# A decoder trunk's planned order of operations: new planner constants and a second queue for the first weight tile

## The chip, the cores and the metric

The kernel runs on one core of a Trainium2 chip. The metric is device microseconds of one execution, as the median of several runs. A core has TensorE (PE), VectorE (DVE), ScalarE (ACT), GpSimdE (POOL) and SyncE (SP), each with its own instruction queue that it works off in order, and transfer engines (DMA) that move data between memory and the core's own memory.

## The reference

256 tokens of width 1024 go through two layers. Each layer is a half-step SwiGLU feed-forward block, a token mixer and another half-step feed-forward block. The mixer of the first layer (A) is causal sliding-window attention with 16 query heads on 2 key heads, learned sinks and a relative-position bias; that of the second (B) is latent attention with low-rank queries and keys and a rotary part.

```python
def swiglu(h, wg, wu, wd):
    return (jax.nn.silu(h @ wg) * (h @ wu)) @ wd
...
    for i in range(DEPTH):
        x = x + 0.5 * swiglu(rmsnorm(x, ffn_norm1[i]), ffn1_wg[i], ffn1_wu[i], ffn1_wd[i])
        h = rmsnorm(x, mix_norm[i])
        j = i // N_MIXERS
        if i % N_MIXERS == 0:
            x = x + sliding_window_attention(h, positions, rel_bias, a_w_in[j], a_q_gain[j],
                                             a_k_gain[j], a_sinks[j], a_w_out[j])
        else:
            x = x + latent_attention(h, positions, b_w_in[j], b_q_norm[j], b_kv_norm[j],
                                     b_w_uq[j], b_w_ukv[j], b_q_gain[j], b_k_gain[j], b_w_out[j])
        x = x + 0.5 * swiglu(rmsnorm(x, ffn_norm2[i]), ffn2_wg[i], ffn2_wu[i], ffn2_wd[i])
```

All is float32; the hidden width of the feed-forward blocks is 2816.

## The kernel before, in words

The tokens stand as two tiles of 128 (t = 0 and 1). Weights come as tiles of 128 x 1024 float32 (512 KB) into `raw`, five buffers. Each is split into a high part `whi` (ScalarE, L402) and a low part `wlo` (VectorE, L397), eight buffers each; a product of two float32 matrices is then three matmuls in TensorE's rounded float32: high by high, high by low, low by high (L735 to L737 for projections, L783 for the down projection, L854 for gate and up). A feed-forward block runs in 11 chunks of 256 hidden columns: gate and up, tanh and products on ScalarE and VectorE, the cast `pT` and its rest `t` of the result, and the down projection of the chunk before. The cast of h (L868) may run on ScalarE or VectorE.

In layer A, keys and queries are projected, normalised (squares on ScalarE, a sum on VectorE, a power on GpSimdE, L647) and transposed (L688); then for each t, key head and parity come scores (L1063), a softmax (row maximum L896 and the scaling of p L941 on VectorE, exponentials L920 on ScalarE), transposes of p (L688), the product with v (L1089) and the output projection. Layer B does the same with its own lines: L1180 and L1209 make keys and queries, L1260 and L1262 scores, L1274 the product with v. The scaling of p may run on VectorE, GpSimdE or ScalarE.

No one writes the order by hand. The program first records every operation with its engine, an estimated cost, what it reads and writes (`Plan.op`), and then `Plan.run` orders them: at each step it takes, of all operations that are ready, the one with the earliest start by its model plus a penalty `pen`. `PEN` holds penalties by kind of operation and engine, `SKEW` how far t = 1 is put behind t = 0 in each stage, `WINDOW` how far in a stream it looks ahead, `PENW` the penalty of weight splits. `pe_time` models TensorE's clock: time is cut into ticks, and a tick runs at half rate where too little work was booked in the tick before. `o.dense` says how much an operation counts there (scores and products with v count for less). Where the plan leaves TensorE idle, `fill` puts filler matmuls of the identity (L1348), whose results nobody reads. The instructions stand in each engine's queue in the order found.

All weight transfers, and those of x (L345, two halves for each t), are issued from SP (L394). The first weight tile comes in two halves, each as two transfers: four in all.

Of the kernel before, what the change touches and what calls it, by code (L numbers as in the profile page):

```python
# [41 lines left out]
WINDOW = 20  # L42
RESERVE = 1
SKEW = [1, 7, 8, 3, 4, 2]
# [3 lines left out]
PENW = [1.0, 0.5, 0.7, 0.7, 0.6, 1.0]  # L48
PEN = {
    "C": {"DVE": -0.4, "POOL": -0.2},  # L50
    "CT": {"*": 0.05, "DVE": -0.1, "PE": -0.05},
    "G": {"DVE": -1},
    "KT": {"PE": 0.05},
    "KV": {"*": -0.2, "ACT": -0.1, "DVE": -0.1, "PE": 0.05},
    "N": {"ACT": 0.4, "DVE": -0.1, "PE": -0.05, "POOL": 0.2},
    "Oa": {"PE": -0.05},
    "PT": {"PE": -0.2},
    "PTB": {"*": 0.05, "PE": -0.6},
    "PV": {"*": -0.6, "DVE": -0.05, "PE": -0.2},
    "PVB": {"*": 0.6, "PE": 0.2},  # L60
    "Q": {"ACT": 0.1, "DVE": 0.1},
    "QB": {"PE": 0.4},
    "QTB": {"*": 0.1},
    "S": {"ACT": 0.1, "PE": -0.2},
    "SB": {"PE": 0.05},
    "T": {"*": -0.05, "PE": -0.1},
    "X": {"DVE": 0.4},
    "Xa": {"DVE": -0.1},
    "Xb": {"DVE": -0.2},
}  # L70
POOLPEN = 1
FILLMIN, FILLFROM = 0.5, 2.0
BSPEN = 2.0
# [27 lines left out]
class Plan:  # L101
# [22 lines left out]
    def op(self, eng, cost, fn, r=(), w=(), seq=None, pen=0.0, prio=None, tail=0.0, name=None):  # L124
# [29 lines left out]
        o.dense = 0.6 if nm[:1] in ("S", "P") and eng == "PE" and nm[1:2] != "T" else 1.0  # L154
# [64 lines left out]
    def pe_time(self, s, cost, book=False, dense=1.0):  # L219
# [87 lines left out]
def kernel(  # L307
# [24 lines left out]
    def c_act(n, extra=0.0):  # L332
        return 0.1 + 0.00083 * n + extra
# [43 lines left out]
    def weight(key, n, srcs):  # L377

        if key not in wtiles:
# [7 lines left out]
            for j in range(parts):  # L387
# [204 lines left out]
    def bias_ops(t, grp):  # L592
# [9 lines left out]
        for i0 in (0, 4) if t else ():  # L602
# [10 lines left out]
            op("ACT", 8 * c_act(P, 0.02), fn, [nj, qidx, df, hd], [m, (steps, i0)], pen=BSPEN, name="bs")  # L613
# [78 lines left out]
    def norm(t, key, gi):  # L692
# [11 lines left out]
        for hf in range(2):  # L704
# [4 lines left out]
            for k2 in (2 * hf, 2 * hf + 1):  # L709
# [12 lines left out]
                op(AV, (0.48, 0.4), high, [b, (gc, int(gi > 1))], xk(0, t, k2), name=name)  # L722
# [8 lines left out]
        op("POOL", 0.97, rs, [ss, mhalf], [rstd, var], name=name)  # L731
# [22 lines left out]
    def ffn(key, gi, wg, wu, wd, extra=None, last=False):  # L754
# [44 lines left out]
        def first(t):  # L799
# [8 lines left out]
            op("POOL", 0.35, consts, [rstd], [hr, q2], name=f"hr{key}.{t}")  # L808
# [29 lines left out]
        for c in range(1, NCH):  # L838
            hthi, htlo = ht[c] = buf("pT", [P, 2, NT * P], F32R), buf("t2", [P, 2, NT * P], F32R)
            for fb in range(2):  # L840
# [27 lines left out]
                op(AV, (c_act(FC, -0.05), c_dve(FC)), copy_scaled(lambda hthi=hthi, fb=fb: hthi[:, fb], lambda h=h: h.t),  # L868
# [233 lines left out]
    def mixer_b(t):  # L1102
# [98 lines left out]
        def queries(g):  # L1201
# [28 lines left out]
            op("DVE", 0.6, rope, [qb, K["ssq", t], K["ccq", t]], [(qn, 1), tmp], name=name)  # L1230
# [166 lines left out]
```

## Time and profile before

| | |
|---|---|
| three timed runs | 952.58, 953.30, 954.87 us; median 953.3 |
| the profiled execution | 955.77 us |
| its span, first to last instruction | 954.0 us |
| its mean granted TensorE clock | 0.994 |

The page of a profile gives busy times by engine and line. A window table gives, for a stretch of time, the busy time of each engine, the granted clock of TensorE as a share of 2.4 GHz, and what the transfers moved. A timeline lists instructions with start and duration, merged where the same one repeats, and in brackets how long the engine had been idle and what ended that. A float32 matmul whose operands are not rounded appears as two records for scores, fillers and keys. PE stands for matmuls, PEld for the loads of their stationary operand.

### The profile page before, as it was taken

Reading aid. Unit: us, or ns where it says so; the run is one execution under the profiler, and the core shown is the slowest. Engines: PE = TensorE matmul, PEld = TensorE weight load, DVE = VectorE, ACT = ScalarE, POOL = GpSimd, SP = SyncE. Lnnn points to the kernel's source line nnn. Section 1 sums busy time; section 2 is a strip of 40 time slices with the busy share of each in tenths; the row PEclk is TensorE's granted clock in tenths of the full one; section 3 lists DMA queues with packets and bytes.
Section 4 is the critical chain, followed back from the end, with each engine's and each line's share of the span. In section 5 each row is a group of like instructions: output and inputs, shape, how many; then the busy total and the mean of one; then the engine's idle time right before and its main releaser. Section 6 shows DMA issues by size and latency. Waiting matters only on the chain.

```text
span 954.0 us, 16706 instructions
## 1 busy us (share of the span) xinstructions
PE 940.6 (99%) x6378; PEld 842.6 (88%) x6378; DVE 654.8 (69%) x1283; ACT 490.4 (51%) x854; POOL 49.4 (5%) x117
## 2 busy tenths in 40 slices
PE   8999999999999999999999999999999999999998
PEld 6999999988668999999989999998868889999997
DVE  6787777786767765666686656566698677565662
ACT  7484666355556543544464434443587445344540
POOL 2000000013000000000010000000431000000000
PEclk9999999999799999999999999999999999999999
DMA  8766556545115666565655656656201477556441
GB/s 287 232 209 209 167 176 192 165 133 179 43 45 178 219 200 199 166 200 165 201 172 173 204 178 187 203 162 199 95 1 46 141 238 225 192 177 209 159 140 45
DMA packets 119632, 160.07 MB, mean 168 GB/s; under 512 B 9264, under 2 KB 102912, under 8 KB 119552
## 3 DMA queue, kind: packets, MB, share of 16 engines
q1 hardware_dynamic: 119552, 159.00, 53.2%
q8 instruction: 50, 0.82, 0.4%
q14 instruction: 30, 0.25, 0.1%
HBM read 157.92 MB, written 1.05 MB: 167 GB/s over the span
## 4 chain that ended last, share of the span: by engine, by line
PE 93%; DVE 3%; DMA 2%; ACT 1%; issue 1%; SPq 0%; POOL 0%; DVEq 0%; ACTq 0%
PE w L854 47%; PE acc L783 26%; PE w L688 3%; PE acc L735 2%; PE acc L737 2%; PE acc L736 2%; PE w L735 1%; PE w L737 1%; PE w L736 1%; DMA raw<-in_ffn_wu_dram 1%; DVE wlo L397 1%; PE w L1262 1%; PE w L1209 1%; PE w L1063 1%; PE acc L1089 1%; PE acc L1274 1%
## 5 line engine op out<-in xcount | busy, mean ns | idle before, releaser
L854 PE MATMUL w<-xs,whi 128*128 128x256 f32 x2560 | 458.3, 282 | 0.0
L854 PEld LDWEIGHTS w<-xs,whi 128*128 128x128 f32 x2560 | 395.4, 189 | 3.4 <-ACT whi L402 0.2
L397 DVE TENSOR_TENSOR wlo<-raw,whi 128x1024 fp32r<-128x1024 f32 (+2 forms) x295 | 352.4, 1215 | 53.1 <-ACT whi L402 50.0
L402 ACT CAST whi<-raw 128x1024 fp32r<-128x1024 f32 (+2 forms) x295 | 303.8, 1042 | 121.1 <-PE acc L783 68.1
L854 PE MATMUL w<-xs,wlo 128*128 128x256 f32 x1280 | 360.5, 282 | 0.8 <-DVE wlo L397 0.8
L854 PEld LDWEIGHTS w<-xs,wlo 128*128 128x128 f32 x1280 | 241.0, 188 | 1.0 <-DVE wlo L397 1.0
L862 ACT ACTIVATE th<-h 128x256 f32<-128x256 f32 x80 | 33.5, 419 | 202.6 <-DVE h L860 202.6
L783 PE MATMUL acc<-wlo,pT 128*128 128x512 f32 x352 | 113.5, 396 | 0.0
L783 PE MATMUL acc<-whi,pT 128*128 128x512 f32 x352 | 113.5, 396 | 0.0
L783 PE MATMUL acc<-whi,t 128*128 128x512 f32 x352 | 113.3, 396 | 0.0
L860 DVE TENSOR_TENSOR h<-w,rb 128x256 f32<-128x256 f32 x80 | 34.0, 424 | 112.3 <-PE w L854 111.2
L783 PEld LDWEIGHTS acc<-whi,t 128*128 128x128 f32 x352 | 66.1, 188 | 16.3
L783 PEld LDWEIGHTS acc<-wlo,pT 128*128 128x128 f32 x352 | 66.1, 188 | 15.4
L783 PEld LDWEIGHTS acc<-whi,pT 128*128 128x128 f32 x352 | 63.4, 189 | 12.0
L870 DVE TENSOR_TENSOR t<-h,pT 128x256 fp32r<-128x256 f32 x80 | 34.0, 425 | 28.4 <-ACT pT L656 27.6
L864 DVE SCALAR_TENSOR_TENSOR th<-th,w 128x256 f32<-128x256 f32 x80 | 33.5, 419 | 26.5 <-ACT th L862 26.5
L656 ACT CAST pT<-h 128x256 fp32r<-128x256 f32 x61 | 24.8, 406 | 32.2 <-DVE h L866 32.0
L735 PE MATMUL acc<-whi,xs 128*128 128x512 f32 x96 | 39.9, 415 | 0.1
L737 PE MATMUL acc<-whi,xs 128*128 128x512 f32 x96 | 38.2, 398 | 0.4 <-DVE xs L674 0.4
L736 PE MATMUL acc<-wlo,xs 128*128 128x512 f32 x96 | 37.8, 394 | 0.0
L920 ACT ACTIVATE p<-p,st 128x128 f32<-128x128 f32 (+1 forms) x64 | 31.2, 491 | 10.2 <-DVE st L911 6.6
L735 PE MATMUL w<-whi,xs 128*128 128x512 f32 (+2 forms) x96 | 36.2, 377 | 0.0
(190 smaller groups left out, 814.6 us busy)
## 6 DMA issues: line engine op xcount, KB each, us to landing
raw<-in_ffn_wd_dram SPq DMA_DIRECT2D x88, 512.0 KB, 4.7
raw<-in_ffn_wg_dram SPq DMA_DIRECT2D x175, 256.0 KB, 3.9
raw<-in_ffn_wu_dram SPq DMA_DIRECT2D x175, 256.0 KB, 4.3
raw<-in_a_w_in_dram SPq DMA_DIRECT2D x10, 512.0 KB, 4.5
raw<-in_a_w_out_dram SPq DMA_DIRECT2D x8, 512.0 KB, 4.1
raw<-in_b_w_out_dram SPq DMA_DIRECT2D x8, 512.0 KB, 3.8
raw<-in_b_w_in_dram SPq DMA_DIRECT2D x4, 416.0 KB, 3.5
whi<-in_b_w_uq_dram SPq DMA_DIRECT2D x4, 384.0 KB, 3.1
```

The costliest lines, as they stand in the source:

```text
L397: V.tensor_tensor(out=lo[:, c], in0=raw[:, c], in1=hi.t.bitcast(F32)[:, c], op=ALU.subtract)
L402: op("ACT", c_act(m), lambda c=c: A.copy(out=hi[:, c], in_=raw[:, c]), [(raw, key_)], [(hi, key_)], seq="wh", pen=pen, prio=pr, name="W")
L735: T.matmul(o, lhsT=hi, rhs=wh, start=start, stop=False)
L736: T.matmul(o, lhsT=hi, rhs=wl, start=False, stop=False)
L737: T.matmul(o, lhsT=lo, rhs=wh, start=False, stop=stop)
L783: T.matmul(acc[nh].t, lhsT=a[:, ft, t0 : t0 + P], rhs=wt[:, nh * 512 : (nh + 1) * 512], start=(c == 0 and ft == 0 and i == 0), stop=(final ...
L854: T.matmul(o, lhsT=wt[:, sl], rhs=xs[:, p, :, kt], start=(kt == j == i == 0), stop=(kt == KT - 1 and j == 1 and i == 2))
L860: op("DVE", 0.345, lambda h=h, ps=ps: V.tensor_tensor(out=h.t, in0=ps[:, :FC], in1=rb.t, op=ALU.mult), [ps, rb], [h], name=nm)
L862: op("ACT", c_act(FC, 0.05), lambda th=th, h=h: A.activation(th.t, h.t, AF.Tanh, scale=0.5), [h], [th], name=nm)
L864: op("DVE", 0.345, lambda th=th, ps=ps: V.scalar_tensor_tensor(out=th.t, in0=th.t, scalar=1.0, in1=ps[:, :FC], op0=ALU.add, op1=ALU.mult), ...
L870: op("DVE", 0.36, lambda h=h, hthi=hthi, htlo=htlo, fb=fb: V.tensor_tensor(out=htlo[:, fb], in0=h.t, in1=hthi[:, fb].bitcast(F32), op=ALU. ...
L920: A.activation(pv(i), pv(i), AF.Exp, bias=nm[:, i : i + 1], scale=1.0 if scale is None else scale[:, i : i + 1], accum_out=den[:, i : i + 1],)
```

## The change

It sets other constants of the planner (window, skews, penalties), counts scores and products with v as 0.5 in place of 0.6 in the clock model and asks 0.42 of a tick in place of 0.374 for the full rate, sets some costs anew, and issues the first weight tile's four transfers from ScalarE's queue. Since the order comes from the planner, all queues come out in another order. Lines after the change stand nine higher than before (L1348 is L1357).

```diff
-WINDOW = 20
+WINDOW = 26
 RESERVE = 1
-SKEW = [1, 7, 8, 3, 4, 2]
+SKEW = [1, 7, 5, 7, 8, -4]
...
-PENW = [1.0, 0.5, 0.7, 0.7, 0.6, 1.0]
+PENW = [1.0, 0.1, 0.7, 0.3, 0.4, 1.0]
 PEN = {
-    "C": {"DVE": -0.4, "POOL": -0.2},
-    "CT": {"*": 0.05, "DVE": -0.1, "PE": -0.05},
...
+    "C": {"DVE": -0.4, "POOL": -0.8},
+    "CT": {"*": 0.05, "DVE": 1.1, "PE": -0.05, "POOL": 0.15, "ACT": 0.15},
...
-POOLPEN = 1
-FILLMIN, FILLFROM = 0.5, 2.0
-BSPEN = 2.0
+POOLPEN = 0
+FILLMIN, FILLFROM = 0.35, 2.0
+BSPEN = 0.5
...
-        o.dense = 0.6 if nm[:1] in ("S", "P") and eng == "PE" and nm[1:2] != "T" else 1.0
+        o.dense = 0.5 if nm[:1] in ("S", "P") and eng == "PE" and nm[1:2] != "T" else 1.0
...
-            rate = 1.0 if self.ticks.get(k - 1, 0.0) >= 0.374 * TICK else 0.5
+            rate = 1.0 if self.ticks.get(k - 1, 0.0) >= 0.42 * TICK else 0.5
...
-                def load(j=j):
+                def load(j=j, q=nc.sync if len(wtiles) else nc.scalar):
                     for f, ap in srcs:
                         v = f(raw[:, :n])
-                        nc.sync.dma_start(out=v if parts == 1 else v[:, j : j + 1], in_=ap if parts == 1 else ap[:, j : j + 1])
+                        q.dma_start(out=v if parts == 1 else v[:, j : j + 1], in_=ap if parts == 1 else ap[:, j : j + 1])
...
-            op("ACT", 8 * c_act(P, 0.02), fn, [nj, qidx, df, hd], [m, (steps, i0)], pen=BSPEN, name="bs")
+            op("ACT", 2.73, fn, [nj, qidx, df, hd], [m, (steps, i0)], pen=BSPEN, name="bs")
...
-                op(AV, (0.48, 0.4), high, [b, (gc, int(gi > 1))], xk(0, t, k2), name=name)
+                op(AV, (0.51, 0.52), high, [b, (gc, int(gi > 1))], xk(0, t, k2), name=name)
...
-        op("POOL", 0.97, rs, [ss, mhalf], [rstd, var], name=name)
+        op("POOL", 1.12, rs, [ss, mhalf], [rstd, var], name=name)
...
-            op("POOL", 0.35, consts, [rstd], [hr, q2], name=f"hr{key}.{t}")
+            op("POOL", 0.5, consts, [rstd], [hr, q2], name=f"hr{key}.{t}")
...
-                op(AV, (c_act(FC, -0.05), c_dve(FC)), copy_scaled(lambda hthi=hthi, fb=fb: hthi[:, fb], lambda h=h: h.t),
+                op(AV, (c_act(FC), c_dve(FC)), copy_scaled(lambda hthi=hthi, fb=fb: hthi[:, fb], lambda h=h: h.t),
...
-            op("DVE", 0.6, rope, [qb, K["ssq", t], K["ccq", t]], [(qn, 1), tmp], name=name)
+            op("DVE", 0.47, rope, [qb, K["ssq", t], K["ccq", t]], [(qn, 1), tmp], name=name)
```

**The start.** SP's queue before; `x_64` and `x_65` are the tokens of t = 0 and 1, `raw` a weight tile, and a row with 128x256 is one of the four transfers of the first tile:

```order
L1393 UNCONDITIONAL_BRANCH
L345 DMA grow<-in_ffn_norm_dram 16x128
L345 DMA x_64<-in_x_dram 128x512 x2
L394 DMA raw<-in_ffn_wg_dram 128x256
L394 DMA raw<-in_ffn_wu_dram 128x256
L394 DMA raw<-in_ffn_wg_dram 128x256
L394 DMA raw<-in_ffn_wu_dram 128x256
L394 DMA raw<-in_ffn_wg_dram 128x2x256
L394 DMA raw<-in_ffn_wu_dram 128x2x256
L345 DMA x_65<-in_x_dram 128x512 x2
```

SP's queue now:

```order
L1402 UNCONDITIONAL_BRANCH
L354 DMA grow<-in_ffn_norm_dram 16x128
L354 DMA x_64<-in_x_dram 128x512 x2
L403 DMA raw<-in_ffn_wg_dram 128x2x256
L403 DMA raw<-in_ffn_wu_dram 128x2x256
L354 DMA x_65<-in_x_dram 128x512 x2
```

ScalarE's queue now, where the four stand ahead of its table load and its first squares of x (`junk`):

```order
L1402 UNCONDITIONAL_BRANCH
L403 DMA raw<-in_ffn_wg_dram 128x256
L403 DMA raw<-in_ffn_wu_dram 128x256
L403 DMA raw<-in_ffn_wg_dram 128x256
L403 DMA raw<-in_ffn_wu_dram 128x256
L709 ACT_TABLE_LOAD
L709 ACTIVATE junk,ss_139<-x_64 128x512 x2
L411 CAST whi<-raw 128x512 x2
```

The second weight tile and x of t = 1 have moved up by four transfers in SP's queue. On TensorE the transposes of x of t = 1's first half now stand ahead of the first projection.

**Layer A.** TensorE's queue before, from the transposes of the normalised keys (`kna`) of t = 0; `kTa,q_2869` are scores of t = 0, `kTa,q_2938` of t = 1, `p` is a softmax:

```order
L688 MATMUL w<-ident,kna 128x128 x2
L1348 MATMUL w<-ident 128x128 x3
L1063 MATMUL w<-kTa,q_2869 128x128 x16
L688 MATMUL w<-ident,kna 128x128 x2
L1348 MATMUL w<-ident 128x128 x5
L1063 MATMUL w<-kTa,q_2938 128x256 x6
L688 MATMUL w<-ident,p 128x128 x8
L1063 MATMUL w<-kTa,q_2938 128x256 x2
L1089 MATMUL acc_3170<-pT,va_96 64x512 x2
```

TensorE's queue now, from the last third of a projection's second half of keys and values (`w<-whi,xs`); 2804 are the queries of t = 0, `acc_3000` is a query projection of t = 1:

```order
L745 MATMUL w<-wlo,xs 128x256
L746 MATMUL w<-whi,xs 128x256
L744 MATMUL w<-whi,xs 128x256
L745 MATMUL w<-wlo,xs 128x256
L746 MATMUL w<-whi,xs 128x256
L1072 MATMUL w<-kTa,q_2804 128x128 x4
L697 MATMUL w<-ident,t_2971 128x128 x4
L744 MATMUL acc_3000<-whi,xs 128x512
L745 MATMUL acc_3000<-wlo,xs 128x512
L746 MATMUL acc_3000<-whi,xs 128x512
L744 MATMUL acc_3000<-whi,xs 128x512
L745 MATMUL acc_3000<-wlo,xs 128x512
```

The scores of t = 0 have moved up: eight stand ahead of a dozen 256-wide projection matmuls of the keys and values of t = 1, four more ahead of a dozen 512-wide ones, after which the first transposes of p come, then another dozen and the last four. No filler is left in layer A (8 before).

**Layer B.** TensorE's queue before, at the last scores (L1262) of t = 1, the products with v (L1274) and what follows; `acc0_8455` is the output projection (rows with buffer numbers):

```order
L1260 MATMUL w_8384<-S8_7843,S4_8142 128x128
L1262 MATMUL w_8384<-S4_8142 128x128
L1274 MATMUL acc0_8351<-pT_8356,q40_7779 64x128 x4
L1348 MATMUL w_8424<-ident_66 128x128 x13
L688 MATMUL w_8424<-ident_66,p_8372 128x128 x2
L688 MATMUL w_8424<-ident_66,p_8381 128x128 x2
L688 MATMUL w_8442<-ident_66,p_8372 128x128 x2
L688 MATMUL w_8442<-ident_66,p_8381 128x128 x2
L735 MATMUL acc0_8455<-whi_7747,xs_69 128x512
```

TensorE's queue now, at the last scores of t = 1:

```order
L1269 MATMUL w_8396<-S8_7835,S4_8291 128x128
L1271 MATMUL w_8396<-S4_8291 128x128
L1357 MATMUL w_8408<-ident_66 128x128 x2
L697 MATMUL w_8408<-ident_66,p_8277 128x128 x2
L697 MATMUL w_8408<-ident_66,p_8341 128x128 x2
L697 MATMUL w_8419<-ident_66,p_8277 128x128 x2
L697 MATMUL w_8419<-ident_66,p_8341 128x128 x2
L744 MATMUL acc0_8430<-whi_7740,xs_69 128x512
```

Thirteen fillers have become two here; in all of layer B there are 8 in place of 18. Of 26 scalings of p on VectorE in layer B 14 are left, six more are on ScalarE and six on GpSimdE. In the feed-forward blocks all 80 casts of h now stand on VectorE, in place of 19, and none of 61 is left on ScalarE.

## Rows read from the trace of the kernel before

**Rows 1.** Page, busy time by engine, share of the span, instructions:

```profile
PE 940.6 (99%) x6378; PEld 842.6 (88%) x6378; DVE 654.8 (69%) x1283; ACT 490.4 (51%) x854; POOL 49.4 (5%) x117
```

**Rows 2.** Windows: length, busy PE, PEld, DVE, ACT, POOL, clock, DMA share, GB/s:

```profile
312.00:480.00 168.00, 168.00 (x1181) 156.79 (x1180) 108.72 (x155) 76.70 (x97) 0.13 (x1) 1.00 0.63 192
...
680.00:740.00 60.00, 57.93 (x401) 44.35 (x399) 51.93 (x200) 47.08 (x131) 19.00 (x28) 1.00 0.11 33
```

**Rows 3.** Timeline of the start: start, duration, engine, instruction, idle before:

```profile
0.72 1.28 ACT L700 ACT_TABLE_LOAD   x1 [0.72 <-PEq L1383]
2.10 0.43 SPq L394 DMA_DIRECT2D raw<-in_ffn_wg_dram  x1
3.83 0.63 ACT L700 ACTIVATE junk<-x 128x512 bf16<-128x512 f32 x1 [1.82 <-DMA x<-in_x_dram]
...
4.99 0.94 SPq L345 DMA_DIRECT2D x<-in_x_dram  x2
8.91 0.50 PE L736 MATMUL w<-wlo,xs 128*128 128x512 f32 x1 [0.94 <-DVE wlo L397]
10.46 1.25 PE L688 MATMUL w<-ident,x 128*128 128x128 f32 x8 [0.83 <-DMA x<-in_x_dram]
11.47 0.48 PE L735 MATMUL w<-whi,xs 128*128 128x512 f32 x1
```

**Rows 4.** Timeline of TensorE in layer A:

```profile
236.83 0.83 PE L1348 MATMUL w<-ident 128*128 128x128 f32 x6
237.69 2.88 PE L1063 MATMUL w<-kTa,q 64*128 64x128 f32 x32
...
241.04 1.38 PE L1348 MATMUL w<-ident 128*128 128x128 f32 x10
242.82 2.10 PE L1063 MATMUL w<-kTa,q 64*128 64x256 f32 x12 [0.40 <-DVE kTa L1030]
244.85 0.72 PE L688 MATMUL w<-ident,p 128*128 128x128 f32 x4
247.22 0.63 PE L688 MATMUL w<-ident,p 128*128 128x128 f32 x4 [1.64 <-DVE st L932]
```

**Rows 5.** Window of TensorE alone: length, busy, clock:

```profile
249.20:259.50 10.30, 10.30 (x28) 0.50 0.16 51
```

**Rows 6.** Chain of waits: start, time, what:

```profile
256.24 0.43 PE acc L735
...
263.23 0.24 PE acc L735
```

**Rows 7.** Timeline of TensorE in layer B, its fillers:

```profile
682.10 0.83 PE L1348 MATMUL acc<-ident 128*128 128x128 f32 x6
...
723.17 0.61 PE L1348 MATMUL w<-ident 128*128 128x128 f32 x4
...
731.41 3.17 PE L1348 MATMUL w<-ident 128*128 128x128 f32 x26
```

**Rows 8.** Windows of the start, one us each:

```profile
4.00:5.00 1.00, 1.00 (x6) 1.00 (x7) 0.00 (x1) 0.97 (x3) 0.00 (x0) 1.00 0.66 166
...
12.00:13.00 1.00, 1.00 (x6) 0.80 (x5) 1.00 (x5) 0.77 (x3) 0.00 (x0) 1.00 1.11 374
```

**Rows 9.** Lines of VectorE, 680 to 740 us: count, busy, mean ns, idle before:

```profile
L941 DVE TENSOR_SCALAR p<-p,st 128x256 f32<-128x256 f32 x14 | 4.0, 348 | 0.1
...
L941 DVE TENSOR_SCALAR p<-p,st 128x128 f32<-128x128 f32 x12 | 2.8, 279 | 0.0
```

**Rows 10.** Timeline of GpSimdE, a copy at the start:

```profile
3.04 0.29 POOL L504 COPY mask<-causal 128x128 f32<-128x128 f32 x1
```

**Rows 11.** Lines of GpSimdE, 680 to 740 us:

```profile
L647 POOL TENSOR_TENSOR st<-st,mhalf 128x4 f32<-128x4 f32 x16 | 16.2, 1018 | 27.1 <-DVE st L1217 13.1 <-DVE st L933 9.7 <-DVE st L1186 4.2
```

**Rows 12.** Casts of h, 312 to 480 us: min/median/max ns, first and last start:

```profile
L656 ACT CAST pT<-h x11: 402/406/407, 317.6 to 473.4; 128x256 fp32r<-128x256 f32 x11
L660 DVE CAST pT<-h x9: 294/295/296, 331.4 to 467.2; 128x256 fp32r<-128x256 f32 x9
```

More of the change, by code (lines that the diff above doesn't have):

```diff
@@ L47 @@
 TICK = 10.24 / 3
-PENW = [1.0, 0.5, 0.7, 0.7, 0.6, 1.0]
+PENW = [1.0, 0.1, 0.7, 0.3, 0.4, 1.0]
 PEN = {
-    "C": {"DVE": -0.4, "POOL": -0.2},
-    "CT": {"*": 0.05, "DVE": -0.1, "PE": -0.05},
-    "G": {"DVE": -1},
-    "KT": {"PE": 0.05},
-    "KV": {"*": -0.2, "ACT": -0.1, "DVE": -0.1, "PE": 0.05},
[L55 to L69, printed above, removed]
-}
-POOLPEN = 1
-FILLMIN, FILLFROM = 0.5, 2.0
-BSPEN = 2.0
+    "C": {"DVE": -0.4, "POOL": -0.8},
+    "CT": {"*": 0.05, "DVE": 1.1, "PE": -0.05, "POOL": 0.15, "ACT": 0.15},
+    "D": {"*": -0.6},
+    "G": {"DVE": 0.2, "POOL": 0.6, "ACT": 0.15},
+    "H": {"ACT": -0.35, "DVE": 0.15},
[5 rows of a table added]
+    "Ob": {"ACT": -0.6, "POOL": 0.6},
+    "PT": {"PE": -0.05, "DVE": 0.2, "POOL": -0.15, "ACT": -0.3},
+    "PTB": {"*": -0.1, "PE": -0.6, "ACT": 0.6, "DVE": -0.05},
+    "PV": {"*": -0.6, "DVE": -0.05, "PE": -0.2, "POOL": 0.75, "ACT": 0.15},
+    "PVB": {"*": 0.45, "PE": 0.2, "ACT": 1.2, "DVE": 0.05, "POOL": -0.6},
+    "Q": {"ACT": -1.1, "PE": -0.05, "POOL": -0.3},
+    "QB": {"PE": 0.1, "ACT": 0.05, "*": 0.05},
+    "QT": {"DVE": 0.2, "PE": -0.3},
+    "QTB": {"*": 0.15, "ACT": -0.45, "DVE": 0.05, "POOL": -0.15},
+    "R": {"PE": 0.2, "ACT": -0.45, "POOL": 0.3, "DVE": -0.3},
+    "S": {"ACT": 0.1, "PE": -0.05, "POOL": 0.15, "*": 0.05},
+    "SB": {"PE": 0.05, "POOL": -0.3, "ACT": -0.1},
+    "T": {"*": 0.1, "PE": -0.1, "DVE": 0.3, "ACT": 0.6},
+    "X": {"DVE": 0.4, "PE": -0.05, "ACT": 0.6},
+    "Xa": {"DVE": -0.15, "PE": 0.3, "ACT": 0.6, "POOL": -0.6},
+    "Xb": {"DVE": -0.2, "PE": -0.3, "POOL": 0.1},
+    "bias": {"POOL": 0.05, "DVE": 0.3, "*": 0.05, "ACT": 0.6},
+    "bs": {"DVE": -0.15},
+    "hrf": {"PE": 1.05, "DVE": 0.15, "POOL": 0.15, "ACT": 0.3},
+}
+POOLPEN = 0
+FILLMIN, FILLFROM = 0.35, 2.0
+BSPEN = 0.5
 class Buf:
```

4 rows, old and new, of the table PEN are left out of this document.

## The prediction

> **What bounds the kernel now.** I read the page's busy times first. TensorE works 940.6 of 954.0 us [rows 1], so an edit counts only where it shortens TensorE's own queue. In a feed-forward stage there is nothing to take: from 312 to 480 us TensorE is busy 168.00 of 168.00 us at full clock [rows 2]. The 40 slices and the windows by stage then lead to three places where time is lost without the page's busy share showing it.
>
> The first is the start. The timeline shows TensorE waiting at 8.91 us for the low half of the first weight tile and at 10.46 us for x, and running without a gap only from 11.47 us [rows 3].
>
> The second is attention layer A. From 236.83 us the queue holds filler matmuls (L1348), score matmuls, fillers again, then a wait [rows 4]; and from 249.2 to 259.5 us the granted clock is 0.50, that is 1.2 of 2.4 GHz, with TensorE busy in all 10.30 us [rows 5]. What it did just before was fillers, 64-row score matmuls and a wait of 1.64 us [rows 4]. One projection matmul of the same shape took 0.43 us there and 0.24 us after it [rows 6].
>
> The third is attention layer B. Between 680 and 740 us VectorE is busy 51.93 of 60.00 us and ScalarE 47.08 [rows 2], and TensorE fills 36 records with filler matmuls, 26 of them in one stretch of 3.17 us [rows 7].
>
> **The change, part by part.** The computation is the same: no matmul, softmax or weight instruction is added or dropped, only filler matmuls, and the choice of ScalarE, VectorE or GpSimdE for copies that may run on either. All terms below are against the profiled execution, 955.77 us (span 954.0); the median of the three timed runs is 953.3, or 2.5 us lower, so the sum is shifted by that at the end.
>
> *Start.* Four transfers of the first weight tile leave SP's queue for ScalarE's. On SP the first was issued at 2.10 us and x1 only at 4.99 [rows 3]. Six transfers stood between, 2.89 us or 0.48 us each; four of them are gone, so x1 is issued 1.9 us sooner. All of that is the upper end. On ScalarE the four stand ahead of its table load (1.28 us, from 0.72 [rows 3]): at SP's 0.43 us each they end at 2.45, the load at 3.73, and the first square of x0, which now starts at 3.83 when x0 lands, is not delayed. If ScalarE took twice as long, it would be 1.7 us late; that is the lower end, less than zero. What makes me take less than the upper end is that x0 now shares the transfer engines with the first weight tile, and that VectorE's own queue (gains, x high and low parts, two weight halves) runs nearly closed from x0's landing to the wait that ended at 8.91. I put x0 0.5 us late, x1's transposes ahead of the first projection, and then a wait of about 1 us on VectorE for t=1. TensorE then has its first 24 projection matmuls done about **0.9 us** sooner (bounds -1.0 and +1.9). After that it is fed as before.
>
> The row says that the engines had room: DMA share 0.66 and 166 GB/s from 4 to 5 us, 1.11 and 374 GB/s from 12 to 13 [rows 8]. The Trainium skill, "DMA: Bandwidth & Descriptors", section "Issuing engines are not separate DMA queues", speaks against the edit: transfers started by different engines run on the same 16 DMA engines and interleave, and a second issuer saves only issue time, usually small beside the transfer. By that rule the term would be near 0 and the forecast 0.9 us higher. The row at 4 us, less than two thirds full while SP was issuing, is why I keep the term.
>
> *Attention layer A.* In the old order both fillers and all early scores stand in a row behind the last projection. In the new order no filler stands in layer A, and between the first scores and the first transposed p stand 12 matmuls of the 256-wide and 12 of the 512-wide projection, then 12 more 512-wide ones before the next p. From 236.83 us to the end of the wait at 247.22 are 10.39 us [rows 4]. The useful work inside is 2.88 and 2.10 us of scores, 0.72 us of transposes and about 0.5 us of k transposes: 6.2 us, so 4.2 us are filler or idle. The half-speed stretch of 10.3 us, all busy, did 5.15 us' worth of work [rows 5]: 5.1 us lost. Together 9.3 us.
>
> How much comes back? Before, 7.16 us passed from the first score (237.69) to the first transposed p (244.85) [rows 4]. The new order puts 4 scores, 8 transposes, 24 projection matmuls and another 4 scores between those two points: 0.7 + 1.0 + 12 x 0.12 + 12 x 0.24 + 0.7 = 6.7 us. A 512-wide matmul takes 0.24 us [rows 6] and a 256-wide one half of that; four scores are 8 of the 32 records of 2.88 us [rows 4]; a transpose is as large as a filler, 0.12 us [rows 7]. So the cover is 0.5 us short there, and similar at three later joints (q for t=1 waits for a GpSimdE power, the first p of t=1, the last PV). I take 4 joints of 0.6, 2.4 us, as left, and **6.9 us** as the gain. Bounds: 9.3 if nothing waits, and -5.1 if the waits move, the half-speed stretch stays and a second one joins it. I choose nearer the upper end, since TensorE has real work where it had fillers.
>
> *Attention layer B.* 18 filler matmuls become 8, that is 36 records become 16; at 3.17/26 = 0.122 us each [rows 7] 2.4 us of filler go. What they covered must be shorter or the wait shows as idle time. VectorE, the busiest of the waited-for engines, loses 12 of 26 scalings of p (26 cost 4.0 + 2.8 us, 0.26 each [rows 9]): 3.1 us less in its queue. Six of them go to ScalarE and six to GpSimdE. The trace shows no such scaling on GpSimdE. A copy of 128x128 took 0.29 us there, and its power on 4 columns 1.02 us [rows 10, 11]: 1.7 to 6.1 us for six, hidden unless such a one is the last before a p transpose. I take 0.4 us each, since a scaling of 128x128 is nearer the copy. Gain **2.7 us**, between the 2.4 of the fillers and the 3.1 of VectorE; bounds -5.1 (a half-speed stretch like A's comes here instead) and +5.
>
> *Feed-forward.* 61 casts of h move from ScalarE (406 ns) to VectorE (295 ns) [rows 12], 18 us on VectorE over four stages. In the window from 312 to 480 us, 11 casts would add 3.2 us to 108.72 of 168 [rows 2, 12]. The cover is VectorE's idle third, and the down projection runs a chunk later. I count 0; without cover it costs at most the casts behind which TensorE waits, 1 us. The changed costs (L613, L722, L731, L808, L868, L1230 and others) issue nothing themselves; they act through the order.
>
> Sum: 0.9 + 6.9 + 2.7 = 10.5 us, 955.8 - 10.5 = 945.3 in the profile's terms and **942.8 us** in those of the median.
>
> **The rivals.**
> *The half-speed stretch stays.* For it: the scores and PV of t=1 still stand close together in A, and before the clock fell TensorE had waited only once for long, 1.64 us [rows 4, 5]. Against: projections now stand among the scores. Price 5.1 us: 947.9.
> *The other engines set the pace.* ScalarE's exponentials and VectorE at 87% in layer B [rows 2] finish no sooner, so fillers turn into idle time and the start is hidden as well; only the clock comes back. 953.3 - 5.1 = 948.2.
> *Both.* The order does not do what it says: the vector wait and the half clock merely move. Only the start's 0.9 is left: 952.4.
> *Slower: the clock falls more often.* In layer B, with 36 records of filler, the clock stayed at 1.00 [rows 2, 7]; the new order has 20 records fewer. One half-speed stretch costs 5.1 us wherever it lies. With the start, half of A's 4.2 us and B's 2.7 kept, one stretch as before gives 953.3 - 5.7 = 947.6, two 952.7, three 957.8. From the third on it is slower; the profile for it has the clock row below 1 in both layers.
>
> **How the numbers follow.** The forecast has 0.62, the half-speed stretch alone 0.15, the pace of the others 0.10, both 0.08, the third stretch 0.05. About 0.3%, 2.9 us, is what a measurement of this kernel can tell from none: faster is below 950.4, slower above 956.2. The first three cases are faster (0.87), but the tails of the second and third cross 950.4, so 0.84; "both" and those tails give 0.11; 0.05 slower. The forecast's own range is 938 to 947: 942.8 less 4.7 if A's joints and B's waits close (2.4 + 2.3), plus 4 if the start gives nothing and the joints cost twice as much. The 8 in 10 reach up past the second and third cases and 1 us below the forecast's own range: 937 to 951.
>
> **What would show it.** Start: the first matmul of the unbroken run at about 10 to 10.5 us instead of 11.47, and x1 landed before 9.5. Layer A: no L1357 filler between 200 and 300 us, no window with clock 0.50 there, and the last projection of A about 8 us sooner. Layer B: 16 filler records, VectorE's p scalings down, the end of B another 3 us ahead. Feed-forward: TensorE busy all the time, as from 312 to 480 us now. The forecast is wrong if the clock row falls below 1 again in either layer, or if waits on softmax (TensorE waiting for p or its power) sum to more than 5 us in A.

## The result and the profile after

| | before | after |
|---|---|---|
| median, us | 952.94 | 942.37 |
| all runs, us | 952.19 to 954.87 (4) | 942.03 to 943.43 (4) |
| ratio | | 0.9888, 95% interval 0.9871 to 0.9905 |
| profiled execution, its span, us | 955.77, 954.0 | 942.21, 940.4 |
| its mean granted clock | 0.994 | 0.999 |

The forecast was 942.8 us, its range 937 to 951. The number came out. Of the terms behind it only the feed-forward blocks' was right in size, and the profiles and experiments show how errors that lay against each other made the sum hold all the same. *Before* and *after* name the two kernels, e1 to e12 the experiments, which follow further down.

The page's busy times of the kernel after, against [rows 1]: TensorE is still the bound, with 8.3 us less busy time in 13.6 us less span. About 5 us of the 8.3 are the half-clock stretch of the execution before, in which the same work kept TensorE busy for longer.

```profile
PE 932.3 (99%) x6344; PEld 837.3 (89%) x6344; DVE 663.5 (71%) x1306; ACT 479.6 (51%) x821; POOL 53.3 (6%) x127
```

The timeline of the start (start, duration, engine, instruction, idle before in brackets), against [rows 3]:

```profile
0.72 0.42 ACTq L403 DMA_DIRECT2D raw<-in_ffn_wg_dram  x1
...
2.62 1.28 ACT L709 ACT_TABLE_LOAD   x1 [2.62 <-issue]
...
3.33 1.78 SPq L354 DMA_DIRECT2D x<-in_x_dram  x2
4.60 0.63 ACT L709 ACTIVATE junk<-x 128x512 bf16<-128x512 f32 x1 [0.70 <-DMA x<-in_x_dram]
...
6.58 1.11 PE L697 MATMUL w<-ident,x 128*128 128x128 f32 x4 [0.83 <-DMA x<-in_x_dram]
...
10.44 0.60 PE L697 MATMUL w<-ident,x 128*128 128x128 f32 x4
10.79 0.48 PE L744 MATMUL w<-whi,xs 128*128 128x512 f32 x1
```

x1 is issued at 3.33 us instead of 4.99. But x0 is later: the first square of x0 starts at 4.60 us instead of 3.83, and the transposes of its second half only at 6.58. The unbroken run of useful matmuls begins with x1's transposes, at 10.44 us. With x0 the clock came late too: by the clock record of the traces it was at 1.00 from 10.39 us on, in the execution before from 6.90. (Before its first record a window prints 1.00 as well, but the 14 filler records from 7.48 us took 3.12 us, 0.22 each, nearly twice the 0.12 of [rows 7].)

The timeline of TensorE in layer A, against [rows 4], and below it windows of TensorE alone (length, busy, clock, DMA share, GB/s), against [rows 5]:

```profile
228.94 1.71 PE L1072 MATMUL w<-kTa,q 64*128 64x128 f32 x16
230.58 0.66 PE L697 MATMUL w<-ident,t 128*128 128x128 f32 x4
230.99 0.37 PE L744 MATMUL w<-whi,xs 128*128 128x256 f32 x1
...
232.59 1.16 PE L1072 MATMUL w<-kTa,q 64*128 64x128 f32 x8
233.68 0.66 PE L697 MATMUL w<-ident,t 128*128 128x128 f32 x4
234.09 0.48 PE L744 MATMUL acc<-whi,xs 128*128 128x512 f32 x1
...
236.95 0.60 PE L697 MATMUL w<-ident,p 128*128 128x128 f32 x4
...
256.14 1.13 PE L1072 MATMUL w<-kTa,q 64*128 64x256 f32 x4 [0.24 <-ACT pT L665]
```

```profile
228.00:249.00 21.00, 21.00 (x126) 1.00 0.23 74
249.20:259.50 10.30, 10.06 (x47) 1.00 0.62 199
```

Scores and projections now alternate, no filler stands in layer A, the only wait of its attention on another engine's result is 0.24 us, and the clock stays at full speed (2.4 GHz) where it had been at 0.50.

The window of all engines in a feed-forward stage (PE, PEld, DVE, ACT, POOL, clock) for [rows 2], then layer B: fillers for [rows 7] and the lines of the scalings of p for [rows 9]:

```profile
312.00:480.00 168.00, 168.00 (x1169) 156.13 (x1168) 114.63 (x176) 74.14 (x94) 1.35 (x5) 1.00 0.62 188
```

```profile
674.34 0.83 PE L1357 MATMUL acc<-ident 128*128 128x128 f32 x6
...
718.24 0.94 PE L1357 MATMUL w<-ident 128*128 128x128 f32 x6
...
720.79 0.61 PE L1357 MATMUL w<-ident 128*128 128x128 f32 x4
```

```profile
L950 DVE TENSOR_SCALAR p<-p,st 128x256 f32<-128x256 f32 x8 | 2.4, 346 | 0.0
...
L950 DVE TENSOR_SCALAR p<-p,st 128x128 f32<-128x128 f32 x6 | 1.4, 278 | 0.0
```

On GpSimdE the scaling that the trace of before had not shown:

```profile
L954 POOL TENSOR_SCALAR p<-p,st 128x128 f32<-128x128 f32 x6 | 2.1, 371 | 5.9 <-DVE st L942 4.5 <-PE w L1271 1.3
```

Sixteen filler records are left of 36. In the feed-forward window VectorE took 5.9 us more (114.63 against 108.72), 3.2 of it by 11 more casts as forecast, the rest by other work that now falls into this window; TensorE is busy 168.00 of 168.00 us as before.

To see where time went, I cut each trace at starts of matmul records that every kernel has. *Start* ends at the 48th record of L735 to L737; *FF 0* at the last gate or up matmul (L854) of the first feed-forward block; *A* at the last of the second block, so it holds layer A; *middle* at layer B's first key matmul (L1180); *B* at the first down projection of the last block (L783). The lengths in us:

| kernel | start | FF 0 | A | middle | B | rest | span |
|---|---|---|---|---|---|---|---|
| before | 21.64 | 172.21 | 276.89 | 212.17 | 93.20 | 177.89 | 954.00 |
| e6, order of before | 21.88 | 172.99 | 271.86 | 212.17 | 93.31 | 177.89 | 950.10 |
| e2, first tile from ScalarE | 21.23 | 172.45 | 273.19 | 212.17 | 93.73 | 177.90 | 950.67 |
| e3, before without fillers | 24.15 | 172.21 | 272.89 | 212.17 | 94.73 | 177.90 | 954.04 |
| after | 22.07 | 172.21 | 268.44 | 212.43 | 87.37 | 177.91 | 940.43 |
| e5, order of after | 21.79 | 173.16 | 267.99 | 212.42 | 87.38 | 177.90 | 940.64 |
| e1, first tile from SP | 24.37 | 172.27 | 268.66 | 212.23 | 87.38 | 177.90 | 942.80 |
| e9, x0 from both queues | 24.54 | 172.51 | 268.06 | 212.43 | 87.38 | 177.91 | 942.82 |
| e4, after without fillers | 23.16 | 172.69 | 268.42 | 212.42 | 86.75 | 177.89 | 941.32 |
| e7, skew of B | 21.73 | 172.83 | 267.85 | 212.43 | 89.12 | 177.91 | 941.86 |
| e8, casts on ScalarE | 22.89 | 172.63 | 268.27 | 212.24 | 87.40 | 177.91 | 941.33 |
| e10, p on VectorE | 21.36 | 173.08 | 268.36 | 212.43 | 88.26 | 177.89 | 941.38 |
| e11, durations alone | 21.43 | 173.04 | 273.70 | 212.49 | 95.01 | 178.05 | 953.72 |
| e12, table alone | 21.44 | 185.87 | 268.79 | 212.53 | 91.37 | 177.89 | 957.88 |

Between the two profiled executions, A gave 8.4 us, B 5.8, and the start took 0.4. What became shorter in A and B shows in windows of all engines that are cut at the same marks. Fillers aside, the same matmuls stand between the marks in both kernels. A, in e6 (the order of before in an execution that kept full clock there) and in after:

```profile
194.87:466.73 271.86, 268.37 (x1726) 235.99 (x1725) 187.71 (x387) 139.29 (x251) 13.54 (x26) 1.00 0.53 163
194.28:462.73 268.45, 268.06 (x1711) 235.20 (x1710) 187.85 (x385) 137.95 (x249) 15.22 (x30) 1.00 0.54 165
```

B, in before and in after:

```profile
682.91:776.11 93.20, 90.88 (x567) 71.10 (x566) 76.60 (x249) 61.93 (x154) 20.78 (x33) 1.00 0.26 82
675.15:762.52 87.37, 87.04 (x546) 68.64 (x546) 70.04 (x226) 67.11 (x170) 22.95 (x39) 1.00 0.26 85
```

In A, TensorE's idle time fell from 3.5 us to 0.4 and 2.2 us of fillers went; against that the scores, now among projections, kept TensorE busy 12.5 us in place of 10.4. In B, idle time fell from 2.3 us to 0.3 and fillers from 3.8 us to 1.6; the remaining 1.6 us are the same matmuls, closer behind each other, the transposes above all. So in both layers the gain is waits of TensorE, open or filled, that now have work in them.

But the kernel before does not run alike each time. Beside the experiments it ran 56 times, with a median of 954.05 us, and its time goes with the granted clock of the run:

| granted clock of the run | runs | time, us: lowest, median, highest |
|---|---|---|
| 0.999 to 1.000 | 21 | 950.28, 951.92, 953.45 |
| 0.997 to 0.998 | 11 | 952.52, 953.36, 954.80 |
| 0.994 to 0.996 | 11 | 955.09, 956.13, 958.15 |
| 0.990 to 0.993 | 13 | 957.49, 958.25, 960.55 |

The execution that I had read, at 0.994, belongs to the third row. The kernel after ran at 0.999 or 1.000 in all four runs.

### The profile page after: what moved, and what is told of

It is laid out like the page before. It is cut to its first block, busy times and chain, and to the rows that moved or that the text cites. A ratio compares the mean times of both kernels' runs of the same rounds, so it can differ in the third digit from the quotient of the medians.

```text
span 940.4 us, 16733 instructions
## 1 busy us (share of the span) xinstructions
PE 932.3 (99%) x6344; PEld 837.3 (89%) x6344; DVE 663.5 (71%) x1306; ACT 479.6 (51%) x821; POOL 53.3 (6%) x127
## 4 chain that ended last, share of the span: by engine, by line
PE 96%; ACT 2%; DMA 1%; issue 0%; SPq 0%; DVE 0%; ACTq 0%
PE w L863 48%; PE acc L792 26%; PE w L697 3%; PE acc L744 3%; PE acc L746 2%; PE acc L745 2%; PE w L744 2%; PE w L746 2%; PE w L745 2%; PE w L1072 1%; PE w L1218 1%; DMA raw<-in_ffn_wu_dram 1%; PE acc L1189 1%; ACT p L929 1%; PE acc L1098 1%; PE w L632 1%
## 5 line engine op out<-in xcount | busy, mean ns | idle before, releaser
L792 PEld LDWEIGHTS acc<-whi,pT 128*128 128x128 f32 x352 | 63.3, 189 | 12.1 <-ACT pT L665 0.4
L726 DVE SCALAR_TENSOR_TENSOR xs<-w,gcols,xs 128x128 fp32r<-128x128 f32 x96 | 28.9, 345 | 11.6 <-ACT xs L667 9.9
L736 POOL TENSOR_TENSOR var<-ss 128x1 f32<-128x1 f32 x12 | 2.3, 193 | 592.6 <-ACT junk L709 592.6
```

Source lines behind the costliest of these rows:

```text
L726: V.scalar_tensor_tensor(out=xv(1, t)[:, kt], in0=b[:, (kt % 4) * P : (kt % 4 + 1) * P], scalar=gc[:, gi * KT + kt : gi * KT + kt + 1], in ...
L792: T.matmul(acc[nh].t, lhsT=a[:, ft, t0 : t0 + P], rhs=wt[:, nh * 512 : (nh + 1) * 512], start=(c == 0 and ft == 0 and i == 0), stop=(final ...
```

## The experiments

**e5 and e6: the clock model's constants.** In e5 the two constants of after are set back; in e6 those of before are set anew. e5:

```diff
-        o.dense = 0.5 if nm[:1] in ("S", "P") and eng == "PE" and nm[1:2] != "T" else 1.0
+        o.dense = 0.6 if nm[:1] in ("S", "P") and eng == "PE" and nm[1:2] != "T" else 1.0
...
-            rate = 1.0 if self.ticks.get(k - 1, 0.0) >= 0.42 * TICK else 0.5
+            rate = 1.0 if self.ticks.get(k - 1, 0.0) >= 0.374 * TICK else 0.5
```

> The changed kernel with the planner's clock model set back to the old two constants (a softmax matmul counts 0.6 as dense, and the full clock is expected from a share of 0.374 on); the order is found anew, with all other new durations kept. Theory (the order of attention layer A, projections among the scores, comes from the durations, buffers and skews of the new plan; the clock model only decides where fillers stand): layer A stays near 8 us shorter than before, 941 to 945. Rival (the clock model alone moves the projections among the scores): the half-clock stretch of 10 us is back in A, 947 to 950.

> The kernel before with only the two constants of the planner's clock model changed (0.5 and 0.42). Theory (as above): the fillers' number and places change, the scores of A still stand behind the last projections, time within 2 us of before. Rival (the clock model alone): no half-clock stretch in A, 5 us or more shorter.

Measured: e5 941.93 us (940.96 to 944.16, 4 runs), e6 952.42 (951.02 to 960.29, 10 runs). The planner finds the same order on all five engines with either pair of constants, so these are second looks at after and at before. I had expected other places of the fillers; that was wrong. By themselves the two constants do nothing here, in either kernel; the rival, that the clock model alone moves the projections among the scores, has fallen.

What makes e6 worth more: its profile shows the order of before in an execution without the half-clock stretch. A wait in layer A, and the window of [rows 5]:

```profile
248.23 0.63 PE L688 MATMUL w<-ident,p 128*128 128x128 f32 x4 [1.64 <-DVE st L932]
...
249.20:259.50 10.30, 10.30 (x49) 1.00 0.17 53
```

The same queue, at 1.00 in place of 0.50, held 49 records in place of 28 in those 10.30 us. A is then 271.86 us instead of 276.89: 5.0 us of the 8.4 between the two profiles were the clock of one execution. e2, whose order in A is that of before as well, lies between the two, with one short stretch at half clock:

```profile
248.40:251.80 3.40, 3.40 (x10) 0.50 0.00 0
```

From e6 to e5, both at full clock, A gains 3.9 us, B 5.9, and the span 9.5.

**e3 and e4: no fillers.** The fillers' results are read by nobody.

```diff
-    plan.filler = lambda b: T.matmul(b[:, :P], lhsT=ident.t, rhs=ident.t, start=True, stop=True)
+    plan.filler = lambda b: None
```

> The kernel before without its filler matmuls (their result is read by nobody); the order of everything else stays. It asks whether fillers hold the granted clock. Theory A (fillers cover waits and hold the clock, no more): the same waits show as idle time, attention layer A is as long as before or has a longer half-clock stretch, and in layer B the clock falls to 0.50 for about 10 us: 2 to 6 us longer than before. Theory B (fillers delay the work that stands behind them, and the clock does not need them): up to 3 us shorter, no stretch in B at 0.50.

> The changed kernel without its filler matmuls; the order of everything else stays. In layer A there are none, so nothing alters there. In layer B eight fillers (16 records, 2 us) go. If they only cover a wait, the time is within 0.3 us of the changed kernel's and TensorE is idle for those 2 us; if they hold the clock, a stretch at 0.50 appears in B and it is about 5 us longer.

Measured: e3 961.32 us (951.88 to 963.76, 10 runs; ratio to before 1.0067, interval 1.0038 to 1.0096), e4 942.99 (942.77 to 943.14; 0.9889 to before, as after). Eight of e3's ten runs were granted 0.988 or 0.989, lower than any of the 56 runs of before. Its profiled run, one of the other two, has half-clock stretches in both layers:

```profile
246.00:251.40 5.40, 3.85 (x25) 1.00 0.00 0
251.60:254.80 3.20, 3.20 (x10) 0.50 0.00 0
727.00:732.70 5.70, 3.45 (x33) 1.00 0.04 4
732.80:736.10 3.30, 3.30 (x11) 0.50 0.74 225
```

Ahead of them TensorE was busy 3.85 of 5.40 and 3.45 of 5.70 us, with the fillers' places empty. So in the order of before fillers hold the clock, as theory A said; of the 6.4 us by the ratio, a little over the 2 to 6 of that theory, some 2.4 lie at the start (24.15 against 21.64 and 21.88), whose fillers are gone too. In the order of after they are not needed in either layer: e4 ran at 0.999 to 1.000, and B was 0.6 us shorter. Its start was 1.1 us longer than after's; the fillers there are gone too, and full clock came at 14.65 us, not 10.39.

**e1 and e2: the queue of the first weight tile.**

```diff
-                def load(j=j, q=nc.sync if len(wtiles) else nc.scalar):
+                def load(j=j, q=nc.sync):
```

is e1; e2 is the reverse in the kernel before.

> The changed kernel with the four transfers of the first weight tile issued from SP's queue again, at the place in SP's order where the plan put them; nothing else is altered. Theory (the transfers of both queues share the transfer engines, so x0 lands late): x0's halves land near 3.8 and 4.5 us again instead of 4.58 and 6.53, and the weight tile lands a little later; the fourth projection matmul starts between 0.5 us before and 0.5 us after the changed kernel's 11.92, time within 0.1% of 942.4. Rival 1 (ScalarE's queue really saves issue time, as the prediction had it): the first projection is about 0.9 to 1.9 us later, 943.3 to 944.3. Rival 2 (the loss at the start comes from the issue alone): 941.9 or less, with the fourth projection matmul before 11.5 us.

> The kernel before with only the four transfers of the first weight tile issued from ScalarE's queue; its order stays. Theory (shared transfer engines): x0's second half lands after 6 us instead of 4.49, x1 earlier, and the fourth projection matmul starts at 11.5 to 12.5 us: time 0 to 1 us longer than before. Rival (saved issue time): x1 lands 1 us or more sooner and the fourth projection matmul starts by 10.6 us: 0.9 us shorter. Neither changes attention, so a half-clock stretch of about 10 us stays near 249 us, and the time is far from the changed kernel's.

Measured: e1 944.83 us (942.97 to 946.33, 5 runs; 0.9909 of before, interval 0.9886 to 0.9931), all at 0.996 to 0.998; e2 952.45 (12 runs; 0.9998, 0.9976 to 1.0019). In e1 the timeline and two windows of TensorE show the price:

```profile
5.65 3.19 PE L1357 MATMUL w<-ident 128*128 128x128 f32 x14
11.05 0.66 PE L697 MATMUL w<-ident,x 128*128 128x128 f32 x4 [2.20 <-DMA x<-in_x_dram]
```

```profile
9.00:12.20 3.20, 1.15 (x7) 1.00 1.01 356
12.40:15.60 3.20, 3.20 (x12) 0.50 0.93 355
```

TensorE waits 2.20 us for x1, whose transposes the new order puts ahead of the first projection, and behind that the clock is at 0.50 for 3.4 us. The start is 2.4 us longer than the mean of the five profiles with the order and fillers of after and the tile on ScalarE (22.07, 21.79, 21.73, 22.89, 21.36: 21.97), and the median is as much longer (944.83 against 942.37). With FF 0 counted in, which differs by almost 1 us among those five, it is 1.9 (196.64 against 194.75). My theory, no difference, has fallen; rival 1 had the direction, and put at 0.9 to 1.9 us what was about 2. Those five also show how much a start varies with its order and queues unchanged: 1.5 us, the shortest where full clock came first (9.60 us) and the longest where it came last (11.45). So the 0.5 us by which e2's start is shorter in the order of before (21.23 against 21.64 and 21.88) is not told from none, and neither is its timed ratio. The landing of x0 was as the theory said: its second half landed at 4.52 us in e1 and at 6.53 in after, at 6.15 in e2 and at 4.49 in before.

**e9: both halves of x0 first.** One transfer more on ScalarE's queue (`dma` gets a parameter for the queue; excerpt):

```diff
-        dma(0.73, lambda: X[t][:, sl], x[0][t * P : (t + 1) * P, sl], [(X[t], hf)], 0.0, prio)
+        dma(0.73, lambda: X[t][:, sl], x[0][t * P : (t + 1) * P, sl], [(X[t], hf)], 0.0, prio,
+            nc.scalar if (t, hf) == (0, 1) else nc.sync)
```

> The changed kernel with one transfer more on ScalarE's queue: the second half of x0, ahead of the first weight tile; order otherwise the same. In the changed kernel's trace x0's second half was issued at 1.63 us, behind two weight transfers of the other queue, and landed at 6.53 us. Theory (x0's second half is late because weight packets stand before it on the shared transfer engines): it now lands by 5 us, x1 lands 0.3 us or more earlier than 9.08 and 9.76, TensorE's projections start up to 1 us earlier: 941.4 to 942.4. Rival (whatever leaves first takes the same room; the first weight tile is then as much later): within 0.3 us of the changed kernel, with x0 earlier and the weight tile later. Against both: 0.5 us longer or more, if the weight tile's low half becomes the last arrival.

Measured: 944.4 us (942.79 to 947.08, 6 runs; 0.9891 of before, interval 0.9864 to 0.9918). Timeline of ScalarE, then of TensorE:

```profile
3.54 0.33 ACTq L403 DMA_DIRECT2D raw<-in_ffn_wu_dram  x1
3.91 1.28 ACT L709 ACT_TABLE_LOAD   x1 [3.91 <-DMA x<-in_x_dram]
5.20 0.63 ACT L709 ACTIVATE junk<-x 128x512 bf16<-128x512 f32 x1
```

```profile
9.39 0.47 PE L744 MATMUL w<-whi,xs 128*128 128x512 f32 x1
11.85 0.57 PE L745 MATMUL w<-wlo,xs 128*128 128x512 f32 x1 [1.98 <-DVE wlo L406]
```

x0's halves landed at 3.52 and 4.53 us, but the table load now stands behind five issues (the view names x; the fifth issue ended at 3.87), and the weight tile is late: TensorE waits 1.98 us for its low half, and the clock is at 0.50 again, from 12.1 to 15.5 us. x0 landed sooner, the weight tile's last part at 9.38 us in place of 7.34, and the time is 2.0 us longer; the case against both was right.

**e8: casts of h on ScalarE.**

```diff
-                op(AV, (c_act(FC), c_dve(FC)), copy_scaled(lambda hthi=hthi, fb=fb: hthi[:, fb], lambda h=h: h.t),
+                op(AV, (c_act(FC), c_dve(FC)), (lambda e, hthi=hthi, fb=fb, h=h: A.copy(out=hthi[:, fb], in_=h.t)),
```

> The changed kernel with the casts of h that the plan gives to VectorE issued from ScalarE instead, at the same place in the order. Theory (the casts lie beside TensorE's unbroken run): within 0.3% of 942.4, TensorE busy all the time in the feed-forward stages. Rival (the slower ScalarE cast, 406 against 295 ns, is waited for by the down projection): 1 to 4 us longer, with waits of TensorE for hT in the feed-forward stages.

Measured: 942.62 us (941.60 to 943.11), 0.03% from after; the window of the feed-forward stage:

```profile
312.00:480.00 168.00, 168.00 (x1174) 156.34 (x1173) 108.54 (x153) 81.07 (x115) 1.36 (x5) 1.00 0.61 188
```

VectorE 6.1 us less, ScalarE 6.9 more, TensorE without a gap: the casts lie beside it on either engine.

**e10 and e7: what shortens layer B.** e10 puts all 32 scalings of p in layer B on VectorE; e7 sets layer B's skew back. The expectation of e10 speaks of twelve; the edit moves eighteen, all twelve that ScalarE now has and GpSimdE's six, while before had 26 on VectorE and six on ScalarE.

```diff
-                    if e == "DVE":
+                    if e == "DVE" or not sink:
```

```diff
-SKEW = [1, 7, 5, 7, 8, -4]
+SKEW = [1, 7, 5, 7, 4, -4]
```

> The changed kernel with the twelve scalings of p in attention layer B that the plan gives to ScalarE and GpSimdE issued on VectorE instead, at the same places in the order. Theory (VectorE sets the pace of layer B, and its 3.1 us less are the gain there): layer B is 2 to 4 us longer, 944.5 to 946.5. Rival (the gain in B is in the order of the matmuls, one token block's scores among the other's projections): within 0.5 us of the changed kernel.

> The changed kernel with the due-time offset of attention layer B's stage set back from 8 to 4, order found anew. Theory (layer B's 5.8 us come from work of the last feed-forward stage or of the next token block being let in among B's score and PV matmuls, which the offset allows): B loses 2 to 5 us again, 944 to 948. Rival (B's gain comes from the scalings of p taken off VectorE): within 1 us of 942.4.

Measured: e10 942.60 us (942.18 to 943.16), e7 944.53 (943.27 to 945.98). The windows of B in e10 and, for what follows, in e11:

```profile
675.23:763.49 88.26, 87.75 (x547) 68.54 (x546) 73.80 (x244) 63.20 (x158) 20.76 (x32) 1.00 0.27 85
680.66:775.67 95.01, 92.53 (x582) 73.22 (x582) 71.85 (x227) 69.09 (x175) 20.76 (x33) 1.00 0.26 81
```

In e10 B is 88.26 us, 0.9 longer than in after and still 4.9 shorter than in before, though every scaling is on VectorE. e11's VectorE is less busy (71.85 against 73.80 us), its ScalarE little more than that of after (69.09 against 67.11), and its B is the longest of all. So neither the scalings nor the busy time of VectorE or ScalarE sets B's length; the theory has fallen. e7's B is 89.12, 1.7 longer, a little under the 2 to 5 of its theory; the skew is part of what shortens B, not all.

**e11 and e12: durations or table.** The planner's input has two parts: the model (durations and clock constants) and the table found by search (window, skews, penalties, filler limits). Each alone in the kernel before, first tile from SP. e12's edit is the table's lines of the diff; e11's all other lines but the queue, as:

```diff
-            op("ACT", 8 * c_act(P, 0.02), fn, [nj, qidx, df, hd], [m, (steps, i0)], pen=BSPEN, name="bs")
+            op("ACT", 2.73, fn, [nj, qidx, df, hd], [m, (steps, i0)], pen=BSPEN, name="bs")
```

> The kernel before with the changed durations and the two constants of the clock model, but with the old table of the search (window, skews, penalties, filler limits) and the first weight tile on SP's queue; the order is planned anew from these. Theory (the gain is in the search's table; better durations alone do nothing, since the old table was found for the old durations): no better than before, 951 to 957, and a stretch at 0.50 in layer A may be there. Rival (the durations make the plan true, and that is the gain): 943 to 947, near the changed kernel with its first tile on SP (944.8).

> The reverse: the kernel before with the changed table of the search, but with the old durations, the old clock constants and the first weight tile on SP's queue. Theory (durations and table belong together: a table found by search holds for the durations that it was searched with): 948 to 956, between the two kernels or no better than before. Rival (the table's rules are good by themselves, for example projections held back for the scores of layer A): 943 to 946.

Measured: e11 956.08 us (955.33 to 957.37, 10 runs, clock 0.998 to 1.000), e12 961.40 (959.66 to 963.73, 7 runs, clock 0.993 to 0.997); ratios to before 1.0019 (0.9998 to 1.0039) and 1.0063 (1.0041 to 1.0085). Either part alone gains nothing; together, with the tile on SP as here, they gain about 9 us (e1, 944.83). Both rivals have fallen, and e12 is longer than its theory's 948 to 956 as well. e11's clean clock makes it some 4 us longer than before at the same clock. e11 keeps waits and fillers: in B TensorE is idle 2.5 us, and its fillers take 6.2 us, 3.8 in before. e12 has A's gain (268.79) and a third of B's (91.37), and loses 13.7 us in FF 0. Its TensorE timeline there, and a window of all engines:

```profile
66.89 3.37 PE L1357 MATMUL w<-ident 128*128 128x128 f32 x28
70.09 0.51 PE L632 MATMUL w<-bdiag,p 128*128 128x64 bf16 x12
72.20 0.52 PE L632 MATMUL w<-bdiag,p 128*128 128x64 bf16 x12 [1.59 <-DVE p L623]
```

```profile
67.00:73.80 6.80, 4.92 (x60) 4.58 (x59) 4.71 (x16) 6.80 (x21) 0.00 (x0) 1.00 0.00 0
74.00:77.20 3.20, 3.20 (x17) 3.20 (x17) 2.19 (x8) 3.20 (x11) 0.00 (x0) 0.50 0.53 164
77.40:90.90 13.50, 9.98 (x104) 8.72 (x104) 10.76 (x30) 8.84 (x21) 0.00 (x0) 1.00 0.13 41
```

ScalarE is busy 6.80 of 6.80 us with the steps of A's bias; TensorE fills and waits for them (by way of VectorE's L623, which had itself waited 2.0 us for ScalarE's L620), and then (3.5 us, for `wlo`) for a weight split. Two half-clock stretches follow. The new table lets these steps come early (`BSPEN` 0.5 for 2.0), and the old cost, 8 x (0.1 + 0.106 + 0.02) = 1.81 us a group, is too short. The trace has a group every 2.7 us:

```profile
65.90 1.27 ACT L617 ACTIVATE p<-clo,nj 128x128 f32<-128x128 f32 x4
67.08 1.63 ACT L620 ACTIVATE p<-p,df,hd 128x128 f32<-128x128 f32 x4
68.62 1.26 ACT L617 ACTIVATE p<-clo,nj 128x128 f32<-128x128 f32 x4
```

The new cost is 2.73. That this one cost makes all of the 13.7 us was not tried.

## Why the prediction was right or wrong

*The number*, 942.8 against 942.37, is right by a balance of errors, and that they balanced is luck. In the profile's terms the sum was 3.1 us short (945.3 forecast, 942.21 measured); the shift of 2.5 us then took off what the runs of after do not have, since their median, 942.37, is that of the profiled one.

*The shift to the median* is the step that failed. The prediction made its sum against the profiled execution and shifted it by 2.5 us, as if every run of before held the same half-clock stretch and every run of after would lie below its profile. The profiled run was 2.8 us above the median because it held more of it than most. At a clock of 0.999 or more, before takes 951.92 us (21 runs), so of the 10.6 us between the medians 952.94 and 942.37 only about 1.0 was the clock (2.1 of 11.7 by the median of the 56 runs), where I had counted 5.1. In the profiles it was 5.0, as counted.

*Layer A* was forecast at 6.9 us in all, 1.8 of it from fillers and idle time. The mechanism was right: projections among the scores, no filler, one wait of 0.24 us where I had left 4 joints of 0.6. The mis-sized term is this cover: A gained 3.4 to 3.9 us without the clock, since nearly all of the idle time went, while the dearer scores, which the sum did not have, took back some 2 us.

*Layer B* was forecast at 2.7 us from VectorE and the fillers, and gave 5.8. Size and reason were off. The fillers gave 2.2 us, near the 2.4 counted. The sum had nothing for TensorE's open waits, though [rows 2] showed 57.93 busy of 60.00 us: 2.0 us of idle time went, and the same matmuls took 1.6 us less. VectorE's scalings are worth 0.9 us at most (e10) and the skew 1.7 (e7), within those sums. What covers the waits is the order that table and durations give together (e11, e12); which entry makes the rest stays open. GpSimdE's scaling, put at 0.4 us, took 0.371.

*Start*: forecast 0.9 us, measured between 0.4 lost (the two profiles) and 0.1 gained (e6 to e5), which is no difference given the 1.5 us by which such starts vary. The signs that I had named were there, the unbroken run at 10.44 us and x1's first half landed at 9.08 (its second came at 9.76), yet the work was no earlier: the run now begins with x1's transposes, where before three projections had been done by then. I had put x0 0.5 us late; its first half was 0.8, its second 2.0. The room that I read out of [rows 8], 0.66 from 4 to 5 us, was one thin microsecond; the windows from 3 to 4 and from 5 to 6 us of the same trace are full:

```profile
3.00:4.00 1.00, 0.45 (x3) 0.16 (x2) 0.00 (x0) 0.17 (x1) 0.29 (x1) 1.00 0.95 356
5.00:6.00 1.00, 1.00 (x6) 1.00 (x5) 1.00 (x4) 0.30 (x2) 0.44 (x3) 1.00 1.06 307
```

And the term held two things at once: the new order costs 2.6 us at the start with the tile on SP (24.37 in e1, one profile, against 21.76, the mean of before and e6), and the queue gives about as much back. The Trainium skill, "DMA: Bandwidth & Descriptors", section "Issuing engines are not separate DMA queues", says that transfers of two issuers interleave on the same engines and that a second issuer saves only issue time, usually little. The first agrees with the traces, where x0's second half landed at 4.49 us before and at 6.53 after. The second does not hold for the new order, in which the queue was worth about 2 us.

*Feed-forward*, 0: right (from before to after middle and rest differ by less than 0.3 us; e8).

*The rivals.* The half-speed stretch did not stay: after and e5 ran at 0.999 or 1.000 each time. The other engines did not set the pace (e10, e11). The third half-clock stretch did not come, nor a first in either layer: no run of after was granted less than 0.999.

*How the sum held*, in the terms of the median: clock about 4 us too much, start about 1 too much, A's cover about 2 and B 3 too little. The forecast's own range had a slip as well: a start that gives nothing and joints at twice the cost are 0.9 + 2.4 = 3.3 us, not 4, so its upper end was 946, not 947.

## What to carry to other kernels

Before a loss is read from one profiled execution, see whether the run's clock and time are those of the other runs: a stretch at half clock may be an event of that run and not of the program. A table found by search belongs to the durations it was searched with; change and test both together. A transfer moved to another queue is weighed by what then lands later, and by what the order puts behind the one that lands sooner.

## What the runs showed of the hardware

One and the same order of instructions was granted 0.990 to 1.000 of the clock, run by run, and took 950.3 to 960.6 us; the order of after was granted 0.999 or 1.000 in all eight runs of after and e5. In layer A, e6 had a wait of 1.64 us for VectorE, as before had, and kept full clock, while e2, in the same order, fell to 0.50 for 3.4 us and before for 10.24: that wait alone does not decide it. What decides between two runs of the same order stays open. The Trainium skill, "TensorE: Matmul & The Clock Gate", section "What's actually happening", says that the gate watches in a free-running manner and does not start anew with the kernel; that fits times that differ run by run, but no run here shows it.
